# A hybrid state-space and attention layer: the u, gate and key products laid by hand as one stream of matmuls between the entry, the tables, the scan and the state outputs

## The chip, the cores and the metric

The kernel runs on one core of a Trainium2 chip. Five engines work side by side: TensorE (PE, matrix products), VectorE (DVE), ScalarE (ACT), GpSimd (POOL) and SyncE (SP, which here only starts DMA transfers). Each takes its own instructions in order, and semaphores hold an instruction back until what it needs is there. The metric is the device time of one execution in microseconds (us).

## The reference, cut to what matters

Two sequences of 512 tokens with 1024 features pass through one encoder layer. A state-space branch and a windowed attention branch are merged by two gates, and a squared-ReLU MLP follows.

```python
h = rms_norm(x, ln1)
q, k, v, u, g_att, g_ssm = split(h @ w_in)          # 1024, 256, 256, 1024, 1024, 1024 columns
k = rms_norm(k, k_gain)
# state-space branch: 64 groups of 16 channels, 64 states, two directions
a = exp(lam * dt);  bb = (a - 1) / lam * b           # complex
h_state[l] = a * h_state[l-1] + bb @ u[l]            # forward, and backward for the other direction
y = Re(c @ h_state), both directions, + d_skip * u
y_ssm = gelu(y) * sigmoid(gelu(y) @ w_glu + b_glu)
mixed = sigmoid(g_att) * y_att + sigmoid(g_ssm) * y_ssm
x = x + mixed @ w_out
out = x + square(relu(rms_norm(x, ln2) @ w_up)) @ w_down
```

## The kernel before, in words

Each fp32 operand of a large product is split into a high part and a rest (names ending in `_hi`, `_lo`, or `hT_0`, `hT_1`), and three products take the place of one. In what follows a "product" is one such matmul of 128x128 weights with 512 columns. A column of 128 output features costs 48 of them (8 slices of the inner dimension, three products each, two sequences). There are 24 columns: eight for u, eight for each gate. The keys take 192 matmuls with 256 columns.

**Entry.** For each of eight blocks of 128 rows: load, square and sum, normalise on DVE (`xn`, L152), turn with eight transposes (L157), split into `hT` (ACT L160, DVE L161). Among these stand some fifty small DVE operations that work out the powers of `a` (`exp_exact`, then `pr`, `pi`); ACT spreads these into `er`, `ei`, `br_p`, `bi_p`.

**Tables.** The 64 groups are done in eight blocks of eight groups (`tables(c)`), each block in two halves q of four groups. For each half DVE makes six operations for `bpre` (three each for real and imaginary part, L385 to L387) and six for `ctab` (L393 to L395). `ctab` goes to DRAM (L396). PE then has three pieces of work for each half: eight lag products of `lbt` with `ctab` (L404, each recorded as two matmuls, 48 output rows), whose results ACT copies to `ks` (L408); eight transposes of `bpre` (L417), copied to `bm` (L419); and eight state inputs `bm` with `u_sb` (L424, also recorded as two each), copied into `h` (L429, L430). `u_sb` (L412) is read back from `u_scr`, to which SP writes a finished u column in eight DMAs (L343). At the end of a block three DMAs store `ks` to `lag_scr` (L435 to L437). SP carries all these transfers in one queue, and the weight loads `c_raw` (L138) of the columns with them. The tile scheduler sets the order on every engine; a u column is emitted two blocks ahead of its tables.

**Scan.** 62 steps of four DVE operations on 128x256 (L533 to L536), each step needing the one before. PE meanwhile runs the gate columns that have no other place.

**State outputs.** 32 steps: copies of `h` into `st`, six logical matmuls (L561, L564), Gelu. From here the order on PE is written by hand: a generator (`gate_stream`, then `key_stream`) hands out products, 12 units after each step, a unit being half a product or one key matmul. What is left of the keys after the last step runs alone. The norm of each key tile follows on ACT, DVE, POOL and DVE (L518 to L524).

**Attention and the rest.** `kn` is read from the `keys` tiles in two DMAs (L806); the v weights `w_in` come in four DMAs (L797), and the query weights in others. The first matmuls of the attention stage stand at L646 and L664.

Of the kernel before, what the change touches and what calls it, by code (L numbers as in the profile page):

```python
# [12 lines left out]
F32 = mybir.dt.float32  # L13
# [50 lines left out]
def hybrid_layer(ctx, tc, x, rel, onehot, ln1, w_qkv, w_ug, q_gain, k_gain, sink, lam_re, lam_im, log_dt,  # L64
                 b_re, b_im, c_re, c_im, d_skip, w_glu, b_glu, w_out, ln2, w_up, w_down, out):
# [42 lines left out]
    bglu_sb = const.tile([P, KT], F32, name="bglu_sb")  # L108
    S.dma_start(bglu_sb, b_glu)
    gain_q = const.tile([P, 1], F32, name="gain_q")  # L110
    gain_k = const.tile([P, 1], F32, name="gain_k")
    S.dma_start(gain_q, q_gain)
    S.dma_start(gain_k, k_gain)
    V.tensor_scalar_mul(gain_q, gain_q, HD ** -0.5)
    nsink = const.tile([P, N_HEADS], F32, name="nsink")
    S.dma_start(nsink, sink.to_broadcast([P, N_HEADS]))
    V.tensor_scalar_mul(nsink, nsink, -1.0)

    def load_block(src, pool):

        hi = pool.tile([P, KT, CB], F32R, tag="w_hi", name="w_hi")
        lo = pool.tile([P, KT, CB], F32R, tag="w_lo", name="w_lo")
        for i in range(4):
            sl = slice(i * 2, i * 2 + 2)
            raw = wpool.tile([P, 2, CB], F32, tag="w_raw", name="w_raw")
            SP.dma_start(raw, src[:, sl, :])
            S.copy(hi[:, sl, :], raw)
            V.tensor_sub(lo[:, sl, :], raw, hi[:, sl, :].bitcast(F32))
        return hi, lo
# [13 lines left out]
    def rows_to_T(xt, gain_bc, pool, dst_hi, dst_lo, col):  # L143
# [8 lines left out]
        V.scalar_tensor_tensor(xn, xt, rs, gain_bc, op0=ALU.mult, op1=ALU.mult)  # L152
        for kq in range(KT // 4):
            ps = tps()
            for i in range(4):
                kk = kq * 4 + i
                PE.transpose(ps[:, i * P:(i + 1) * P], xn[:, kk * P:(kk + 1) * P], ident)  # L157
            psv = ps.rearrange("p (k t) -> p k t", k=4)
            h = dst_hi[:, kq * 4:kq * 4 + 4, col:col + P]
            S.copy(h, psv)  # L160
            V.tensor_sub(dst_lo[:, kq * 4:kq * 4 + 4, col:col + P], psv, h.bitcast(F32))  # L161
# [15 lines left out]
    def proj_rows(ps, w, act, col):  # L177

        for k in range(KT):
            mm3(ps, [t[:, k, col:col + P] for t in act], [t[:, k, :] for t in w], k == 0, k == KT - 1)  # L180

    def gate_column(c, scr, base):

        w = load_column(w_ug[base + c], V.tensor_sub)
        sg = evp.tile([P, NTOK], F32, tag="ev", name="sg")
        for s in range(NSEQ):
            ps = proj_T(w, 0, hT[s])
            S.activation(sg[:, s * HALF:(s + 1) * HALF], ps, AF.Sigmoid)
        SP.dma_start(scr[c], sg)

    def load_qkv(src):

        halves = []
        for e in range(2):
            hi, lo = [cpool.tile([P, KT // 2, CB], F32R, tag=tag, name=name) for tag, name in (("c_hi", "w_hi"), ("c_lo", "w_lo"))]
            for i in range(2):
                sl = slice(i * 2, i * 2 + 2)
                raw = cpool.tile([P, 2, CB], F32, tag="c_raw", name="w_raw")
                SP.dma_start(raw, src[:, e * 4 + i * 2:e * 4 + i * 2 + 2, :])
                S.copy(hi[:, sl, :], raw)  # L200
                V.tensor_sub(lo[:, sl, :], raw, hi[:, sl, :].bitcast(F32))
            halves.append((hi, lo))
        return halves
# [20 lines left out]
    dd = cf.tile([48, GROUPS], F32, name="dd")  # L224
    lbt = cf.tile([P, 2, SB, 48], F32, name="lbt")
    with tc.tile_pool(name="xin", bufs=2, reuse_waits="tile") as xin, tc.tile_pool(name="ssmc", bufs=1) as sc:
# [3 lines left out]
        lr, li, ldt = c64("lr"), c64("li"), c64("ldt")  # L230
        ln1_bc = xin.tile([P, D], F32, name="ln1_bc", bufs=1)
        SP.dma_start(ln1_bc, ln1.to_broadcast([P, D]))
        for t in range(NT):
            xt = xin.tile([P, D], F32, tag="xt", name="xt", bufs=6)
            SP.dma_start(xt, x[t * P:(t + 1) * P, :])
            rows_to_T(xt, ln1_bc, xin, hT[t // 4][0], hT[t // 4][1], (t % 4) * P)
            if t == 0:
                S.dma_start(lr, lam_re)
                S.dma_start(li, lam_im)
                for d in range(2):  # L240
                    S.dma_start(ldt[d * 64:(d + 1) * 64, :], log_dt[d:d + 1, :].to_broadcast([64, GROUPS]))
                SP.dma_start(dd[32:48, :], d_skip)
        V.memset(lbt, 0.0)
# [71 lines left out]
        for src, e_t, b_t in ((pr, er, br_p), (pi, ei, bi_p)):  # L315
# [4 lines left out]
            S.copy(b_t[64:128, :, :], src[64:128, 0:8, :])  # L320

    with tc.tile_pool(name="hst", bufs=1) as hp:
# [10 lines left out]
        def u_column(c):  # L335

            w = load_column(w_ug[U_BLK + c], V.tensor_sub)
            up = evp.tile([P, T, NSEQ, NCHUNK], F32, tag="ev", name="up")
            for s in range(NSEQ):
                ps = proj_T(w, 0, hT[s])  # L340
                S.copy(up[:, :, s, :], ps.rearrange("p (k t) -> p t k", t=T))
            for t in range(T):
                SP.dma_start(u_scr[t, :, c * 8:(c + 1) * 8].rearrange("c g k -> g c k"),  # L343
                             up[:, t].rearrange("p s k -> p (s k)"))

        with tc.tile_pool(name="ssmt", bufs=2) as sp:
            def tables(c):
# [3 lines left out]
                bx = sp.tile([P, 3, SB, CH], F32, tag="bx", name="bx")  # L351
                cx = sp.tile([P, 3, SB, CH], F32, tag="cx", name="cx")
                SP.dma_start(bx[:, 1], b_re[:, gs, :])
                SP.dma_start(bx[:, 2], b_im[:, gs, :])
                SP.dma_start(cx[:, 0], c_re[:, gs, :])
                SP.dma_start(cx[:, 1], c_im[:, gs, :])
                bb = sp.tile([P, 3, SB, CH], F32, tag="bb", name="bb", bufs=1)
                tw = sp.tile([P, 2, SB, CH], F32, tag="tb", name="tw", bufs=1)
                V.tensor_scalar_mul(bx[:, 0], bx[:, 2], -1.0)
                V.tensor_mul(tw, bx[:, 0:2], fi[:, None, gs, None].to_broadcast([P, 2, SB, CH]))  # L360
                V.tensor_mul(bb[:, 1:3], bx[:, 1:3], fr[:, None, gs, None].to_broadcast([P, 2, SB, CH]))
                V.tensor_add(bb[:, 1:3], bb[:, 1:3], tw)
                V.tensor_scalar_mul(bb[:, 0], bb[:, 2], -1.0)
                V.tensor_scalar_mul(cx[:, 1], cx[:, 1], -1.0)
                V.tensor_scalar_mul(cx[:, 2], cx[:, 0], -1.0)
                S.copy(lbt[0:64, :, :, 0:16], bb[0:64, 1:3])
                S.copy(lbt[64:128, :, :, 16:32], bb[64:128, 1:3])
                S.copy(lbt[:, :, :, 32:48], bb[:, 1:3])
                ks = sp.tile([48, SB, 9, CH], F32, tag="ks", name="ks", bufs=1)
                for q in range(SB // SG):  # L370
# [10 lines left out]

                    bpre = sp.tile([P, 2, SG, T, CH], F32, tag="bpre", name="bpre", bufs=1)
                    for ri in range(2):
                        tb = sp.tile([P, SG, 9, CH], F32, tag="tb", name="tb", bufs=1)
                        V.tensor_mul(bpre[:, ri], bc_pow(br_p, T), bc_ch(bb[:, 1 + ri], T))  # L385
                        V.tensor_mul(tb[:, :, 0:T, :], bc_pow(bi_p, T), bc_ch(bb[:, ri], T))
                        V.tensor_add(bpre[:, ri], bpre[:, ri], tb[:, :, 0:T, :])  # L387


                    ctab = sp.tile([P, SG, 2, 9, CH], F32, tag="ctab", name="ctab")  # L390
                    for ri in range(2):
                        tb = sp.tile([P, SG, 9, CH], F32, tag="tb", name="tb", bufs=1)
                        V.tensor_mul(ctab[:, :, ri], bc_pow(er, 9), bc_ch(cx[:, ri], 9))  # L393
                        V.tensor_mul(tb, bc_pow(ei, 9), bc_ch(cx[:, 1 + ri], 9))
                        V.tensor_add(ctab[:, :, ri], ctab[:, :, ri], tb)  # L395
# [4 lines left out]
                    for gp in range(SG // SH):  # L400
                        ps = sps()
                        for g in range(SH):
                            for ri in range(2):
                                PE.matmul(ps[0:48, g * 144:(g + 1) * 144], lbt[:, ri, q * SG + gp * SH + g, :],  # L404
# [36 lines left out]
            for c in range(KT):  # L441
                tables(c)
                if c + 2 < KT:
                    u_column(c + 2)
# [894 lines left out]
```

## Time and profile before

| what | us |
|---|---|
| median of three runs | 1583.43 (1581.27 to 1584.83) |
| the profiled execution | 1583.63 |
| its span in the profile | 1581.9 |
| PE busy in the span | 1499.1 |
| DVE busy | 1128.8 |
| ACT busy | 773.4 |

The span runs from the first to the last instruction, and 1.7 us of the profiled execution lie outside it. Busy time of PE counts an instruction until a modelled end, and consecutive matmuls overlap, so the number of matmuls times the distance between their starts is a better measure of PE's work than the busy sum. The stages by their first and last instructions: entry up to about 40 us, tables 60 to 231, scan 231 to 349, state outputs 349 to 449, the rest of the keys to 457.6. Between 40 and 60 us PE runs the first two u columns.

### The profile page before, as it was taken

To read this page: it belongs to the slowest core of one execution; us is meant where nothing else is said; L and a number is where in the kernel's file an instruction comes from. 1 tells how busy PE (TensorE), PEld (TensorE's weight loads), DVE (VectorE), ACT (ScalarE), POOL (GpSimd) and SP (SyncE) were. 2 spreads that over 40 slices of the span, in tenths; PEclk is the share of its full clock that TensorE was granted. 3 is DMA by queue.
4 is the path that set the end of the run, shared out by engine and by line. 5 is a ranking of instruction groups with operands and counts; after the bars stand their busy time and mean duration, and the time that the engine had idled before them with its cause. 6 is when DMAs were issued, how large, how long until landed. Compare 5 with 4: busy or idle time off the path is not lost.

```text
span 1581.9 us, 21603 instructions
## 1 busy us (share of the span) xinstructions
PE 1499.1 (95%) x7818; PEld 1261.1 (80%) x7818; DVE 1128.8 (71%) x2014; ACT 773.4 (49%) x1365; POOL 168.2 (11%) x294
## 2 busy tenths in 40 slices
PE   4999999999999999998699989999999899999999
PEld 3778878888999988986477777888888778888787
DVE  7899968994544978887866548777777478665553
ACT  5677662224434878787333325455544344433332
POOL 2000002002231233332320000000000000000000
PEclk9999999999999999999799998999999999999999
DMA  4444438626960412214754214444444594445332
GB/s 159 131 140 147 142 125 261 225 100 218 315 195 8 120 60 81 89 55 134 245 160 154 100 73 160 146 146 154 147 155 151 196 363 152 148 157 174 120 120 67
DMA packets 109558, 237.04 MB, mean 150 GB/s; under 512 B 15067, under 2 KB 37723, under 8 KB 109452
## 3 DMA queue, kind: packets, MB, share of 16 engines
q1 hardware_dynamic: 78988, 157.91, 31.2%
q0 software_dynamic: 11008, 39.89, 7.7%
q10 hardware_dynamic: 19456, 37.87, 6.5%
q8 instruction: 62, 1.02, 0.3%
q14 instruction: 44, 0.36, 0.1%
HBM read 165.34 MB, written 81.82 MB: 156 GB/s over the span
## 4 chain that ended last, share of the span: by engine, by line
PE 40%; issue 6%; DMA 2%; DVE 2%; POOL 2%; ACT 1%; POOLq 0%; ACTq 0%; SPq 0%; DVEq 0%
PE bank L166 13%; PE bank L167 13%; PE bank L165 13%; POOL mx L989 1%; PE acc L167 1%; PE acc L166 1%; PE acc L165 1%; DMA w_raw<-in_w_out_dram 0%; DMA k<-in_w_down_dram 0%; DMA fac<-rs_scr 0%; DMA mx<-ga_scr 0%; DVE rn_xn L1068 0%; ACT rn_xn L1064 0%; DMA mx<-mix_scr 0%; DMA mx<-gs_scr 0%
## 5 line engine op out<-in xcount | busy, mean ns | idle before, releaser
L165 PE MATMUL bank<-b_hi,a_hi 128*128 128x512 f32 x448 | 173.8, 391 | 7.3 <-ACT b_hi L1215 7.3
L166 PE MATMUL bank<-b_lo,a_hi 128*128 128x512 f32 x448 | 175.2, 391 | 2.1 <-DVE b_lo L1216 2.0
L167 PE MATMUL bank<-b_hi,a_lo 128*128 128x512 f32 x448 | 174.8, 390 | 0.0
L165 PE MATMUL bank<-act,act 128*128 128x512 f32 x376 | 147.1, 391 | 2.3 <-ACT act L1113 2.3
L1215 ACT CAST a_hi<-d_a 128x1024 fp32r<-128x1024 f32 x56 | 59.0, 1054 | 182.4 <-PE bank L166 175.3
L167 PE MATMUL bank<-act,act 128*128 128x512 f32 x376 | 146.8, 391 | 0.0
L166 PE MATMUL bank<-act,act 128*128 128x512 f32 x376 | 146.8, 390 | 0.0
L1216 DVE TENSOR_TENSOR a_lo<-d_a,a_hi 128x1024 fp32r<-128x1024 f32 x56 | 68.5, 1224 | 106.1 <-ACT a_hi L1215 106.1
L166 PE MATMUL acc<-hT,c_hi 128*128 128x512 f32 x336 | 133.7, 398 | 0.0
L165 PE MATMUL acc<-hT,c_hi 128*128 128x512 f32 x336 | 133.6, 398 | 0.0
L167 PE MATMUL acc<-hT,c_lo 128*128 128x512 f32 x336 | 132.4, 394 | 0.0
L664 PE MATMUL acc<-w_hi,hT 128*128 128x256 f32 x512 | 116.7, 296 | 0.0
L165 PEld LDWEIGHTS bank<-b_hi,a_hi 128*128 128x128 f32 x448 | 84.4, 189 | 25.2 <-ACT b_hi L1215 7.7
L166 PEld LDWEIGHTS bank<-b_lo,a_hi 128*128 128x128 f32 x448 | 84.4, 188 | 21.1 <-DVE b_lo L1216 3.6
L167 PEld LDWEIGHTS bank<-b_hi,a_lo 128*128 128x128 f32 x448 | 84.4, 188 | 17.5
L664 PEld LDWEIGHTS acc<-w_hi,hT 128*128 128x128 f32 x512 | 87.5, 190 | 3.8
L139 ACT CAST c_hi<-c_raw 128x512 fp32r<-128x512 f32 x64 | 39.4, 619 | 94.5 <-DMA c_raw<-in_w_ug_dram 39.8
L165 PEld LDWEIGHTS bank<-act,act 128*128 128x128 f32 x376 | 71.0, 189 | 17.3 <-ACT act L1113 2.7
L166 PEld LDWEIGHTS bank<-act,act 128*128 128x128 f32 x376 | 71.0, 189 | 14.8
L167 PEld LDWEIGHTS bank<-act,act 128*128 128x128 f32 x376 | 70.9, 189 | 15.0
L727 ACT ACTIVATE p<-p,nmx 128x257 f32<-128x257 f32 (+1 forms) x128 | 72.3, 565 | 15.4 <-DVE nmx L721 14.3
L1134 ACT ACTIVATE a<-a 128x512 f32<-128x512 f32 x64 | 40.5, 632 | 73.7 <-DVE a L1128 42.9
(309 smaller groups left out, 3771.7 us busy)
## 6 DMA issues: line engine op xcount, KB each, us to landing
d_a<-a_scr SPq DMA_DIRECT2D x56, 512.0 KB
u_raw<-in_w_up_dram SPq DMA_DIRECT2D x32, 512.0 KB
a_scr<-t ACTq DMA_DIRECT2D x64, 256.0 KB
k<-in_w_down_dram SPq DMA_DIRECT2D x32, 512.0 KB
c_raw<-in_w_ug_dram SPq DMA_DIRECT2D x48, 256.0 KB
a_scr<-a ACTq DMA_DIRECT2D x48, 256.0 KB
ct_scr<-ctab SPq DMA_DIRECT2D x16, 576.0 KB
ctab_in<-ct_scr POOLq DMA_DIRECT2D x16, 576.0 KB, 6.7
```

What stands on the lines that cost most here:

```text
L139: S.copy(hi[:, sl, :], raw)
L165: PE.matmul(ps, a[0], b[0], start=first, stop=False)
L166: PE.matmul(ps, a[0], b[1], start=False, stop=False)
L167: PE.matmul(ps, a[1], b[0], start=False, stop=last)
L664: PE.matmul(self.ps, hT[sq][act][:, k, col:col + P], w[:, k % 4, :], start=i == 0, stop=i == 3 * KT - 1)
L727: S.activation(p, p, AF.Exp, bias=self.nmx[:, h:h + 1], scale=-1.0, accum_out=self.sums[:, h, self.qb:self.qb + 1])
L989: GP.dma_start(t_, scr[m, :, s * HALF:(s + 1) * HALF])
L1134: S.activation(c, c, AF.Relu)
L1215: S.copy(hi, src)
L1216: V.tensor_sub(lo, src, hi.bitcast(F32))
```

## The change

The parameters arrive packed: `lam` (three rows of values) and `vec` (bias, gains, sink, skip) in one DMA each on ACT's queue, in place of eight or nine small ones. The skip values are placed on the host's side of the call as rows of the input array.

All 24 columns and the keys become one generator, `fillers`, and PE's order is by hand from the entry on. `pull(units)` takes so many units from it: 8 ahead of each half of the transposes of row blocks 4 to 7, 144 ahead of the tables, 52 in each half of a table block, 15 (eight products) in each scan step, then 32, and in the 32 state steps whatever is left, spread evenly.

In the tables DVE makes five operations for `bpre` and five for `ctab`, with sums and differences of the parts (`es`, `bs_p`, `bb[:, 2:4]`, `cw`) worked out once. The lag products write to output rows 0 to 63 and 64 to 127 in turn, into one PSUM bank, so that one copy of 128 partitions takes the place of two of 48. `lag_scr` is stored in twelve DMAs for each block instead of three. `u_sb` has one buffer instead of two. The line of relative biases moves into the scan. The number of gate columns whose sigmoid is applied on the spot stays 13.

```diff
-                    for gp in range(SG // SH):
-                        ps = sps()
-                        for g in range(SH):
-                            for ri in range(2):
-                                PE.matmul(ps[0:48, g * 144:(g + 1) * 144], lbt[:, ri, q * SG + gp * SH + g, :],
-                                          ctab[:, gp * SH + g, ri].rearrange("p n c -> p (n c)"),
-                                          start=ri == 0, stop=ri == 1)
-                        gk = q * SG + gp * SH
-                        S.copy(ks[:, gk:gk + SH].rearrange("p g n c -> p (g n c)"), ps[0:48, 0:SH * 144])
...
-                    u_sb = sp.tile([P, SI, NSEQ * NCHUNK], F32, tag="u_sb", name="u_sb")
+                    u_sb = sp.tile([P, SI, NSEQ * NCHUNK], F32, tag="u_sb", name="u_sb", bufs=1)
...
+                    pull(12)
+                    for gp, bm in enumerate(bms):
...
+                        pull(12 if gp == 0 else 16)
+                    ps = ps_o.tile([P, 512], F32, tag="po", name="lag")
+                    for g in range(SH):
+                        for ri in range(2):
+                            for e in range(2):
+                                gk = e * SH + g
+                                PE.matmul(ps[e * 64:(e + 1) * 64, g * 144:(g + 1) * 144], lbt[:, ri, q * SG + gk, :],
+                                          ctab[:, gk, ri].rearrange("p n c -> p (n c)"),
+                                          start=ri == 0, stop=ri == 1)
+                    S.copy(ks[:, q * SH:(q + 1) * SH].rearrange("p g n c -> p (g n c)"), ps[:, 0:SH * 144])
+                    pull(12)
...
-                SP.dma_start(lag_scr[:, gs, 8:15, :], ks[0:16, :, 0:7, :])
-                SP.dma_start(lag_scr[:, gs, 0:7, :], ks[16:32, :, 1:8, :])
-                SP.dma_start(lag_scr[:, gs, 7, :], ks[32:48, :, 8, :])
+                for e in range(2):
+                    kv = ks[e * 64:(e + 1) * 64].rearrange("p (q g) n c -> p q g n c", g=SH)
+                    for q in range(SB // SG):
+                        SP.dma_start(lv[e, :, q, :, 8:15, :], kv[0:16, q, :, 0:7, :])
+                        SP.dma_start(lv[e, :, q, :, 0:7, :], kv[16:32, q, :, 1:8, :])
+                        SP.dma_start(lv[e, :, q, :, 7, :], kv[32:48, q, :, 8, :])
-            u_column(0)
-            u_column(1)
+            pull(144)
             for c in range(KT):
                 tables(c)
...
                 V.tensor_add(h[:, i + 1], t1, t2)
+                pull(15)
...
-                room = 12
-                while room > 0:
-                    cost = next(stream, None)
...
+                pull(-(-phase["units"] // (GROUPS // SH - q)))
```

On SP, at the first table block, before: the u column 0 is stored, and the reads of `u_sb` for the first halves stand ahead of the store of u column 1.

```order
L343 DMA u_scr<-up 8x16x128 x8
L138 DMA c_raw<-in_w_ug_dram 128x512
L412 DMA u_sb<-u_scr 128x512 x2
L343 DMA u_scr<-up 8x16x128 x8
L396 DMA ct_scr<-ctab 128x1152
L412 DMA u_sb<-u_scr 128x512
```

The same place on SP now:

```order
L233 DMA u_scr<-up 8x16x128 x8
L119 DMA c_raw<-in_w_ug_dram 128x512
L233 DMA u_scr<-up 8x16x128 x8
L119 DMA c_raw<-in_w_ug_dram 128x512
L466 DMA ct_scr<-ctab 128x1152
L471 DMA u_sb<-u_scr 128x512
```

The first `u_sb` has moved behind the eight stores of column 1, a weight load and the store of the first `ctab`.

On SP, where the third table block (c = 2) begins, now: the twelve rows of the block before it, of which eight wait for its second half, stand ahead of this block's first `u_sb`. Before, the three rows stood in such a place too, with a second buffer to read into.

```order
L514 DMA lag_scr<-ks 16x2x112
L516 DMA lag_scr<-ks 16x2x16
L515 DMA lag_scr<-ks 16x2x112
L516 DMA lag_scr<-ks 16x2x16 x2
L514 DMA lag_scr<-ks 16x2x112
L515 DMA lag_scr<-ks 16x2x112
L516 DMA lag_scr<-ks 16x2x16
L466 DMA ct_scr<-ctab 128x1152
L471 DMA u_sb<-u_scr 128x512
```

The fourth block (c = 3) has the same arrangement; in the others `u_sb` stands ahead of them.

On SP, at the end of the keys, before, and then now:

```order
L806 DMA kn<-keys 128x1024
L797 DMA w_in<-in_w_qkv_dram 128x1024 x4
L806 DMA kn<-keys 128x1024
L631 DMA bias<-line_scr 128x384 x4
```

```order
L639 DMA w_raw<-in_w_qkv_dram 128x512 x2
L824 DMA kn<-keys 128x1024 x2
L815 DMA w_in<-in_w_qkv_dram 128x1024 x4
L649 DMA bias<-line_scr 128x384 x4
```

Both reads of `kn`, the second of which needs the last key tile, stand ahead of the four `w_in` loads now.

On PE, one half of a table block now (L478 are the transposes, L487 the state inputs, L500 the lag products, L212 the products of the columns; before, these three stood where the scheduler put them, in runs between products):

```order
L478 MATMUL tps<-ident,bpre 128x128 x8
L212 MATMUL acc<-hT_1_103,c_hi 128x512
L212 MATMUL acc<-hT_0_102,c_lo 128x512
L212 MATMUL acc<-hT_0_102,c_hi 128x512
L212 MATMUL acc<-hT_1_103,c_hi 128x512
L212 MATMUL acc<-hT_0_102,c_lo 128x512
L212 MATMUL acc<-hT_0_102,c_hi 128x512
L487 MATMUL sps<-u_sb,bm 128x128 x4
```

Six products follow these four state inputs, then the other four, eight products, the eight lag products and six products.

More of the change, by code (lines that the diff above doesn't have):

```diff
@@ L107, in hybrid_layer @@
     V.memset(neg_half, -0.5)
[L108 to L129, printed above, removed]
+    vec = const.tile([P, 58], F32, name="vec")
+    bglu_sb, gain_q, gain_k, nsink = [vec[:, a:b] for a, b in ((0, 8), (8, 9), (9, 10), (10, 26))]
+    dd = vec[:, 26:58].rearrange("p (x g) -> p x g", g=2)
     def load_column(src, sub):
@@ L152, in rows_to_T, with turn_rows @@
         V.scalar_tensor_tensor(xn, xt, rs, gain_bc, op0=ALU.mult, op1=ALU.mult)
[L153 to L161, printed above, removed]
+        return xn
+    def turn_rows(xn, kq, dst_hi, dst_lo, col):
+        ps = tps()
+        for i in range(4):
+            kk = kq * 4 + i
+            PE.transpose(ps[:, i * P:(i + 1) * P], xn[:, kk * P:(kk + 1) * P], ident)
+        psv = ps.rearrange("p (k t) -> p k t", k=4)
+        h = dst_hi[:, kq * 4:kq * 4 + 4, col:col + P]
+        S.copy(h, psv)
+        V.tensor_sub(dst_lo[:, kq * 4:kq * 4 + 4, col:col + P], psv, h.bitcast(F32))
     def mm3(ps, a, b, first, last):
@@ L175, in proj_T, with load_qkv_half @@
         return ps
[L177 to L203, printed above, removed]
+    def load_qkv_half(src, e):
+        hi, lo = [cpool.tile([P, KT // 2, CB], F32R, tag=tag, name=name) for tag, name in (("c_hi", "w_hi"), ("c_lo", "w_lo"))]
+        for i in range(2):
+            sl = slice(i * 2, i * 2 + 2)
+            raw = cpool.tile([P, 2, CB], F32, tag="c_raw", name="w_raw")
+            SP.dma_start(raw, src[:, e * 4 + i * 2:e * 4 + i * 2 + 2, :])
+            S.copy(hi[:, sl, :], raw)
+            V.tensor_sub(lo[:, sl, :], raw, hi[:, sl, :].bitcast(F32))
+        return hi, lo
     def slot(pool):
@@ new lines, in fillers, with pull @@
+    def fillers():
+        two = [column(i) for i in range(2)]
+        for parts, _ in two:
+            yield from parts[0]
+        for parts, store in two:
+            yield from parts[1]
+            store()
+            load_next()
+        for i in range(2, len(columns)):
+            parts, store = column(i)
+            for part in parts:
+                yield from part
+            store()
+            load_next()
+        yield from key_products()
+    filler = fillers()
+    def pull(units):
+        while units > 0:
+            cost = next(filler, None)
+            if cost is None:
+                return
+            units -= cost
+            phase["units"] -= cost
@@ L361, in tables @@
[L361 to L368, printed above, removed]
@@ L390, in tables @@
-                    ctab = sp.tile([P, SG, 2, 9, CH], F32, tag="ctab", name="ctab")
[L391 to L395, printed above, removed]
+                    tbb = tb[:, :, 0:T, :]
```

276 lines of the change are left out of this document (158 added, 118 removed).

## The prediction, on record before the changed kernel ran

> **What bounds the kernel now.** I read the page first, then the windows by stage, the groups of the tables stage, PE's waits there, and the timeline where stages meet.
>
> ```profile
> span 1581.9 us, 21603 instructions
> PE 1499.1 (95%) x7818; PEld 1261.1 (80%) x7818; DVE 1128.8 (71%) x2014; ACT 773.4 (49%) x1365; POOL 168.2 (11%) x294
> ```
>
> PE is the bound. The change can win only in the 83 us in which PE is idle, in the gaps that a busy share hides, or by making PE's work less. The windows give PE's busy time by stage and the clock granted to it:
>
> ```profile
> 0.00:20.00 20.00, 4.89 (x20) 3.71 (x20) 11.81 (x33) 10.39 (x19) 6.87 (x18) 1.00 0.80 273
> 20.00:40.00 20.00, 14.16 (x58) 11.33 (x57) 17.04 (x38) 11.28 (x20) 3.20 (x5) 0.83 0.16 46
> 60.00:231.00 171.00, 166.06 (x993) 135.16 (x994) 147.61 (x259) 123.24 (x181) 1.12 (x2) 1.00 0.47 147
> 231.00:349.00 118.00, 118.00 (x519) 96.78 (x518) 105.95 (x268) 23.32 (x42) 10.59 (x16) 1.00 0.57 193
> 349.00:458.00 109.00, 109.00 (x768) 101.40 (x767) 49.71 (x73) 42.52 (x78) 27.41 (x41) 1.00 0.71 242
> ```
>
> The columns are length, then busy time and instructions of PE, PEld, DVE, ACT and POOL, then clock, DMA share and GB/s. Scan and state outputs have no idle PE to win. The first 40 us have 21 us of it, the tables stage 4.9. How far matmuls stand apart tells the rest:
>
> ```profile
> 39.04 0.63 PE L167 MATMUL acc<-hT,c_lo 128*128 128x512 f32 x1
> 39.47 0.45 PE L165 MATMUL acc<-hT,c_hi 128*128 128x512 f32 x1
> ...
> 126.21 0.39 PE L165 MATMUL acc<-hT,c_hi 128*128 128x512 f32 x1
> ...
> 128.03 0.39 PE L167 MATMUL acc<-hT,c_lo 128*128 128x512 f32 x1
> 128.34 2.16 PE L404 MATMUL sps<-ctab,lbt 128*48 128x144 f32 x16
> 130.44 1.09 PE L417 MATMUL tps<-ident,bpre 128*128 128x128 f32 x8
> 131.29 0.48 PE L165 MATMUL acc<-hT,c_hi 128*128 128x512 f32 x1
> 131.77 2.05 PE L424 MATMUL sps<-u_sb,bm 128*128 128x128 f32 x16
> 133.66 0.49 PE L417 MATMUL tps<-ident,bpre 128*128 128x128 f32 x3
> ```
>
> Products from 126.21 to 128.03 are eight steps, 0.227 us each (0.43 from 39.04 to 39.47, while the clock was low). Sixteen recorded lag matmuls take 2.10 (128.34 to 130.44), eight transposes 0.85, sixteen state inputs 1.89 with the change of shape behind them (131.77 to 133.66). A change of shape costs: 0.08 from product to lag (0.31 less 0.227), 0.25 from product to state input (0.48 less 0.227).
>
> ```profile
> L166 PE MATMUL acc<-hT,c_hi 128*128 128x512 f32 x118 | 47.9, 406 | 0.0
> L404 PE MATMUL sps<-ctab,lbt 128*48 128x144 f32 x256 | 37.1, 290 | 3.1 <-ACT h L430 2.0 <-DVE ctab L395 1.1
> L424 PE MATMUL sps<-u_sb,bm 128*128 128x128 f32 x256 | 33.3, 282 | 2.4 <-ACT bm L419 2.1 <-ACT ks L408 0.2
> L417 PE MATMUL tps<-ident,bpre 128*128 128x128 f32 x128 | 18.9, 276 | 0.0
> L395 DVE TENSOR_TENSOR ctab<-ctab,tb 128x576 f32<-128x576 f32 x31 | 23.5, 757 | 0.8
> L387 DVE TENSOR_TENSOR bpre<-bpre,tb 128x512 f32<-128x512 f32 x30 | 20.6, 687 | 0.3
> ```
>
> So the tables stage holds some 354 products (3 x 118) at 0.227, 80.4 us; 16 x 2.10 = 33.6 of lag; 16 x 1.77 = 28.4 of state inputs (1.89 less the 0.12 of the change); 16 x 0.85 = 13.6 of transposes. That is 156 us in 171: 15 are lost, about 5.5 in the waits that the rows name, the rest in changes of shape and behind the waits.
>
> **The change, part by part.**
>
> *Entry.* DVE works out its powers first and normalises after that; parameters come in two DMAs. The same 20.9 us of large operations remain on DVE (8 x 1.28 and 16 x 0.69, below), but it starts sooner.
>
> ```profile
> 9.31 0.20 DVE L249 TENSOR_SCALAR ex_r<-ldt 128x64 f32<-128x64 f32 x1 [0.94 <-DMA ldt<-in_log_dt_dram]
> 11.58 1.28 DVE L152 SCALAR_TENSOR_TENSOR rn_xn<-xt,rs,ln_bc 128x1024 f32<-128x1024 f32 x1
> L161 DVE TENSOR_TENSOR hT<-tps,hT 128x512 fp32r<-128x512 f32 x16 | 10.6, 685 | 1.0 <-ACT hT L160 1.0
> ```
>
> Some 36 small operations at about 0.24, 8.6 us, stand ahead of the first `xn`. If `lam` lands near 4.5, `xn` begins near 13 instead of 11.58; but nothing small interrupts it after. I put the end of entry and first columns 3 us ahead: -3.0 (bounds: -4.5; +2 if `lam` lands near 7).
>
> *Tables, waits and shapes.* DVE drops two of twelve operations in each half, 16 x (0.69 + 0.76) = 23 us. That is cover, no path: PE's half is now 26 products (5.9), 2.10, 1.77 and 0.85, 10.6 us, against 7.8 of DVE (147.6 / 16 = 9.2, less 1.45). The 15 us lost go: -15.2. The new order pays its own changes of shape: 32 from product to state input and back at 0.25 + 0.04, 16 from product to lag and back at 0.08 + 0.10, 16 from product to transposes and back at 0.08: +13.5 (6 if most state inputs come without the 0.25).
>
> *Paired lag products.* Two output halves of 64 alternate. If two run at once, 33.6 us become 16.8. No row of this profile has such a pair; L404 uses 48 columns one after another. Bounds: 0 and -16.8; I take -16.8, since nothing but the array is shared by the two halves and their weights, sums and rows are apart. The Trainium skill, TensorEngine Tiling (Array Packing), Key Properties, says that tiles run independently, and that changing the tiling mode drains the array. By the first the saving would be the whole; by the second each return to products costs, and the trace agrees, with 0.08 us going in.
>
> *The first `u_sb`.*
>
> ```profile
> 52.78 5.07 SPq L343 DMA_DIRECT2D u_scr<-up  x8
> 59.23 0.34 SPq L138 DMA_DIRECT2D c_raw<-in_w_ug_dram  x1
> 59.81 0.81 SPq L412 DMA_DIRECT2D u_sb<-u_scr  x2
> 60.67 4.90 SPq L343 DMA_DIRECT2D u_scr<-up  x8
> ...
> 63.91 1.16 PE L424 MATMUL sps<-u_sb,bm 128*128 128x128 f32 x8 [0.23 <-ACT ks L408]
> 56.12 0.59 ACT L341 COPY up<-acc 128x512 f32<-128x512 f32 x1
> ```
>
> Eight stores occupy SP's queue 4.9 us, and now two lots of eight stand ahead. ACT's copy of u column 0 stands behind the `a8` block, near 56 as here; stores to 61.7, weight load, stores to 67, two more issues, `u_sb` at 68, landing at 71 to 72 (4.1 us from 59.81 to the use at 63.91). PE needed it at 63.91; 3 us of entry ahead, it is there at 60.9. That is +11 (6 if the copy comes five us sooner), and no product may pass it. After so long a wait PE starts again at low clock: seven or eight products at 0.43 instead of 0.227, +1.7. The Trainium skill, TensorE: Matmul & The Clock Gate, gives some 3.4 us of idling for the fall to half clock; the row with 0.83 and the 0.43 agree.
>
> *`u_sb` of blocks 2 and 3.* One buffer: its read can start only when the state inputs of the half before are through; in these two blocks the eight `lag_scr` rows in front also wait for that half's lag products, the copy to `ks` and DVE's addition.
>
> ```profile
> 76.96 0.33 SPq L435 DMA_DIRECT2D lag_scr<-ks  x1
> 77.34 0.43 SPq L436 DMA_DIRECT2D lag_scr<-ks  x1
> 77.81 0.44 SPq L437 DMA_DIRECT2D lag_scr<-ks  x1
> 78.76 0.34 SPq L412 DMA_DIRECT2D u_sb<-u_scr  x1
> ```
>
> From the last state input: eight products and the lag 4, copy and addition about 1 by an estimate (two operations like the 0.69 and 0.25 of other rows, on smaller tiles), eight issues at 0.39 3.1, one more 0.4: issue at 8.4, landing 3.5 to 4 later. PE needs it after 14 products, lag, transposes and six products, at 7.5 to 8. So +4.3 each: +8.5 (0 to 11). The six other blocks read ahead of the stores and come in time.
>
> *Scan.*
>
> ```profile
> L533 DVE TENSOR_TENSOR t<-h,a8r 128x256 f32<-128x256 f32 x62 | 26.3, 424 | 6.6 <-DMA c_raw<-in_w_ug_dram 4.7
> ```
>
> DVE needs the whole 118 us again, with its `c_lo` between; PE now has 496 products (112.4), and eight, the lag and six ahead of them and 16 behind. They meet within 2 us: +1.5 (0 to 3).
>
> *State outputs.* Keys are spread to 13.5 units a step and the tail of lone key matmuls goes; PE was full before, so this is worth nothing, covered by the same copies.
>
> *Tail.*
>
> ```profile
> 447.08 2.89 SPq L797 DMA_DIRECT2D w_in<-in_w_qkv_dram  x4
> 461.18 0.50 SPq L806 DMA_DIRECT2D kn<-keys  x1
> ...
> 457.81 0.37 PE L664 MATMUL acc<-w_hi,hT 128*128 128x256 f32 x1
> 461.81 0.39 PE L664 MATMUL acc<-w_lo,hT 128*128 128x256 f32 x1 [1.29 <-DVE w_lo L800]
> ```
>
> Before, `w_in` was issued 10 us ahead of the keys' end. Now it stands behind the `kn` read of 461.18, 3.4 us behind the first attention matmul at 457.81; with 0.5 for that issue and 4.1 to land and be used, as for `u_sb`, plus a cast, that matmul comes some 9 us late. Of the time to 461.81 before, about 2 were lost as well: +7 (4 to 9).
>
> Sum, from the profiled execution's own 1583.6 (0.2 above the median): -3.0 - 15.2 + 13.5 - 16.8 + 11 + 1.7 + 8.5 + 1.5 + 7 = +8.2, so **1591.8**, call it 1592.
>
> **The rivals.**
>
> *The lag halves don't overlap.* For it: what the trace shows of L404 runs strictly one after another, real and imaginary part, 0.13 us each, and no pair is in it. Then +16.8: 1608.6. It decides by the length of eight lag products, 2.1 or 1.05.
>
> *The `u_sb` loads come in time* (the other side). If DVE's early chain lets the copies of u columns 0 and 1 come near 50 to 52, and SP empties its queue faster than the two 5-us rows say, then the first state input finds its data, and in blocks 2 and 3 likewise: -11 - 1.7 - 8.5 gives 1570.6. Before, the one `u_sb` cost no wait (0.23 for ACT at 63.91), which is for it; the two lots of stores are against it. The point is whether `u_sb` is issued by 57.
>
> *The entry gets slower.* The first `xn` waits for `lam` and for a Sin of ACT in the chain ahead of it. If it starts at 17, entry ends 4 late: 1592 + 7 = 1599.
>
> **How the numbers follow.** Chances: forecast 0.45, no overlap 0.2, loads in time 0.22, slow entry 0.13. The forecast alone moves by its bounds about 8 either way, 1584 to 1600. The range 1571 to 1609 leaves out half of the outer two cases, about 0.2. Within 0.2% means within 3.2 us, about what a measurement of this kernel can tell from no change. Faster comes from the loads in time (0.2) and the low end of the others (0.06): 0.26. Same takes the edge of these, 0.08. Slower 0.66.
>
> **What would show it.** In the profile after: first `xn` near 13; eight lag products in 1.05; at the first L487 a wait of about 11 on a DMA, and two of about 4 some 40 and 60 us later; no DVE waits of PE in the tables; the first `w_hi` matmul about 9 us after the last key. The forecast is wrong if the lag cadence stays, if the waits at L487 are missing, or if a wait stands where I have none, above all between scan and state outputs.

## The result, and the profile after

The changed kernel takes 1673.05 us (median of four runs, 1667.72 to 1675.67) against 1582.43 before. The ratio is 1.0566, with a 95% interval of 1.0537 to 1.0596: 90 us slower, where 8 were forecast and the range ended at 1609. The profiled execution's span is 1673.6.

The waits of PE in the profile after, up to the attention stage (engine, tile and line, what was waited for: total us, times, longest):

```profile
PE acc L212 <- ACT sg L227: 61.9, 1, 61.9
PE sps L487 <- DMA u_sb<-u_scr: 20.6, 4, 10.2
PE tps L561 <- DMA rel_sb<-in_rel_dram: 13.3, 1, 13.3
PE tps L141 <- DVE rn_xn L133: 13.0, 1, 13.0
PE acc L682 <- ACT w_hi L817: 5.7, 1, 5.7
...
PE tps L664 <- POOL kd L655: 3.1, 1, 3.1
```

The waits at L487 and, at the start of the attention stage, at L664 and L682 were in the forecast. The first row and the third were not: 75.2 us, and both lie in the scan. The windows of the profile after show the place (length, then busy time and instructions of PE, PEld, DVE, ACT, POOL, then clock, DMA share, GB/s):

```profile
55.00:243.00 188.00, 167.42 (x1059) 138.55 (x1058) 129.51 (x241) 118.81 (x169) 0.00 (x0) 0.95 0.45 141
243.00:262.00 19.00, 15.71 (x68) 12.31 (x66) 13.50 (x34) 3.85 (x7) 7.52 (x11) 1.00 0.78 237
262.00:349.00 87.00, 18.23 (x66) 13.03 (x66) 83.18 (x219) 0.00 (x0) 2.65 (x5) 0.60 0.18 67
349.00:537.00 188.00, 184.91 (x1078) 161.74 (x1079) 59.01 (x86) 58.70 (x105) 26.71 (x41) 0.98 0.54 184
```

From 262 to 349 us DVE runs the scan almost without a break (83.18 of 87 us) while ACT does nothing at all (x0) and PE works 18 of 87 us. Before, PE had no idle time in the scan. ACT's own timeline says what it waits for:

```profile
257.16 0.59 ACT L227 ACTIVATE sg<-acc 128x512 f32<-128x512 f32 x1
257.65 0.61 ACT L120 CAST c_hi<-c_raw 128x512 fp32r<-128x512 f32 x1
349.06 2.01 ACT L578 COPY st<-h 64x512 f32<-64x512 f32 x2 [90.80 <-issue]
350.98 0.57 ACT L562 COPY ohln<-tps 16x512 f32<-16x512 f32 x1
351.46 0.58 ACT L227 ACTIVATE sg<-acc 128x512 f32<-128x512 f32 x1
351.94 0.60 ACT L120 CAST c_hi<-c_raw 128x512 fp32r<-128x512 f32 x1
```

The two copies of `h` into `st` are the first work of the state outputs. They need the last step of the scan, which ends at 349.0, and they stand in ACT's queue ahead of everything ACT still has to do for the products of the scan. So nothing empties the accumulators of the columns and nothing casts the next weights; PE fills what it has and stops. The row says "issue" because the semaphore wait is not resolved to a releaser there. The scan's last row on DVE, 348.48 with 0.43, ends just ahead of the copies:

```profile
348.48 0.43 DVE L557 TENSOR_TENSOR h<-t,t 128x256 f32<-128x256 f32 x1
```

ACT's order shows the same, and could be read before any run (dots stand for rows left out):

```
L227 ACTIVATE sg<-acc 128x512
...
L578 COPY st<-h 64x512
L578 COPY st<-h 64x512
L562 COPY ohln<-tps 16x512
L227 ACTIVATE sg<-acc 128x512
```

In the kernel before, all but a few of the scan's casts and sigmoids stand ahead of those copies, and ACT idles only 9.24 us in front of them:

```profile
339.17 0.62 ACT L139 CAST c_hi<-c_raw 128x512 fp32r<-128x512 f32 x1 [0.23 <-DMA c_raw<-in_w_ug_dram]
349.03 2.12 ACT L554 COPY st<-h 64x512 f32<-64x512 f32 x2 [9.24 <-DVE h L536]
```

What now stands between them is `ohln`, the copy behind the matmul of the relative biases (L561), which the change put into PE's order at scan step 8. The same matmul ran during the scan before, too, and cost no wait there: its table was loaded ahead of the scan, and its copy stood among the scan's own work on ACT. Rows of the kernel before, from SP, PE and ACT:

```profile
227.69 0.33 SPq L454 DMA_DIRECT2D rel_sb<-in_rel_dram  x1
245.15 1.03 PE L458 MATMUL tps<-oh_sb,rel_sb 33*16 33x512 f32 x2
246.21 0.58 ACT L460 COPY ln_sb<-tps 16x512 f32<-16x512 f32 x1 [6.59 <-PE tps L458]
```

Now SP issues that load at 260.00, when PE already waits for it:

```profile
260.00 0.67 SPq L544 DMA_DIRECT2D rel_sb<-in_rel_dram  x1
```

The lag products in pairs, on PE's timeline after:

```profile
160.12 0.39 PE L212 MATMUL acc<-hT,c_lo 128*128 128x512 f32 x1
160.44 1.20 PE L500 MATMUL lag<-ctab,lbt 128*64 128x144 f32 x16
161.57 0.74 PE L212 MATMUL acc<-hT,c_hi 128*128 128x512 f32 x2
```

Sixteen recorded matmuls, which are eight lag products, take 1.13 us (160.44 to 161.57) instead of 2.10.

### The profile page after: what moved, and what is told of

The parts are those of the page before. It is cut to its first block, busy times and chain, and to the rows that moved or that the text cites. A ratio compares the mean times of both kernels' runs of the same rounds, so it can differ in the third digit from the quotient of the medians.

```text
span 1673.6 us, 21682 instructions
## 1 busy us (share of the span) xinstructions
PE 1498.0 (90%) x7818; PEld 1256.0 (75%) x7818; DVE 1111.7 (66%) x1989; ACT 767.7 (46%) x1349; POOL 169.4 (10%) x298
## 4 chain that ended last, share of the span: by engine, by line
PE 37%; issue 6%; DMA 2%; DVE 2%; POOL 2%; ACT 1%; POOLq 0%; ACTq 0%; SPq 0%; DVEq 0%
PE bank L150 12%; PE bank L151 12%; PE bank L149 12%; POOL mx L1007 1%; DMA w_raw<-in_w_out_dram 0%; DMA mx<-mix_scr 0%; DMA mx<-ga_scr 0%; DMA k<-in_w_down_dram 0%; DVE rn_xn L1087 0%; DMA fac<-rs_scr 0%; DMA mx<-gs_scr 0%; ACT rn_xn L1083 0%; PE acc L151 0%; POOL rs L1086 0%; PE acc L150 0%
## 5 line engine op out<-in xcount | busy, mean ns | idle before, releaser
L212 PE MATMUL acc<-hT,c_hi 128*128 128x512 f32 x768 | 257.0, 410 | 61.9 <-ACT sg L227 61.9
L212 PEld LDWEIGHTS acc<-hT,c_hi 128*128 128x128 f32 x768 | 146.0, 193 | 94.5 <-ACT sg L227 62.3
L212 PE MATMUL acc<-hT,c_lo 128*128 128x512 f32 x384 | 157.6, 411 | 0.0
L682 PE MATMUL acc<-w_hi,hT 128*128 128x256 f32 x512 | 119.5, 301 | 5.7 <-ACT w_hi L817 5.7
L121 DVE TENSOR_TENSOR c_lo<-c_raw,c_hi 128x512 fp32r<-128x512 f32 x64 | 43.5, 689 | 95.5 <-ACT c_hi L120 95.1
L682 PEld LDWEIGHTS acc<-w_hi,hT 128*128 128x128 f32 x512 | 89.6, 195 | 9.6 <-ACT w_hi L817 5.9
L212 PEld LDWEIGHTS acc<-hT,c_lo 128*128 128x128 f32 x384 | 74.4, 194 | 17.6 <-issue 2.7
```

Of the source, the lines that this page charges most:

```text
L212: PE.matmul(ps, w[wi][:, k, :], hT[s][hi][:, k, :], start=n == 0, stop=n == 3 * KT - 1)
L682: PE.matmul(self.ps, hT[sq][act][:, k, col:col + P], w[:, k % 4, :], start=i == 0, stop=i == 3 * KT - 1)
```

## The experiments

Every ratio below is to the kernel before in runs on the same chip. The experiments ran on several chips, on which the medians of the kernel before lie between 1584.0 and 1584.7, so times of different runs are compared as they stand. The expectations name the runs by the order in which they ran: first the line of biases behind the scan, second step 20, third the shifted weights, fourth the lag products not alternating, sixth POOL's queue, seventh the tail, tenth all together with the line in the entry. "Theory A" is the reading above: the place of the bias matmul in PE's order makes the place of the state copies in ACT's.

**The line of biases behind the scan.**

```diff
-                if i == 8:
-                    ps = tps()
-                    PE.matmul(ps[0:N_HEADS, :], rel_sb, oh_sb, start=True, stop=True)
...
             pull(32)
+            ps = tps()
+            PE.matmul(ps[0:N_HEADS, :], rel_sb, oh_sb, start=True, stop=True)
```

> The line of relative biases (its matmul, ACT's copy and the two DMAs) is moved from scan step 8 to behind the scan; nothing else changes. Theory A (two state copies of ACT stand ahead of the scan's own ACT work because that matmul stands in PE's order at step 8): ACT works through the scan, the waits of 61.9 and 13.3 us go, and the time is 1673 - 75 - 2 of low clock = 1596, between 1590 and 1602. Rival B (ACT is held by the two buffers of the gate columns or by their stores on SP): the 61.9 us stay and only the 13.3 us go, 1660. Rival C (the wait for the relative table is itself the loss and the rest follows from low clock): like B, 1655 to 1660.

1604.55 us, ratio 1.0125 (1.0109 to 1.0142). Both waits are gone, 68 us of the 90 with them, so the rivals at 1655 to 1660 fall. The result is 3 us above theory A's band. One wait that neither kernel had is longer than that, from PE's waits in this run:

```profile
PE sps L584 <- DMA toep<-toep_scr: 10.2, 1, 10.2
```

**The same matmul at step 20.**

```diff
-                if i == 8:
+                if i == 20:
```

> The same matmul at scan step 20 instead of 8. Theory A: the two state copies move with it, so PE can run twelve more steps of eight products (22 us) before it starves; the 13.3 us wait for the table is gone too, since PE gets there later than 272 us. 1673 - 22 - 13 = 1638, between 1632 and 1645, with a wait of about 50 us that ends when the scan ends. Rivals B and C: no dependence on the step beyond the 13.3 us, 1660 in both places.

1654.19 us (two runs), ratio 1.0441 (1.0419 to 1.0462). From PE's waits:

```profile
PE acc L212 <- ACT sg L227: 49.5, 1, 49.5
...
PE tps L561 <- DMA rel_sb<-in_rel_dram: 6.3, 1, 6.3
```

The wait follows the step, as theory A says and the rivals do not, and its length of about 50 us was forecast. The forecast of the time was 16 us too low, and the upper end of its band 9: the wait shrank by 12.4 rather than 22, and the wait for the table by 7 rather than 13.3. Together 19.4 us, where the medians differ by 18.9. The load of the table moved along with the matmul, from 260.00 to 283.21, which is why that wait did not go. And here the row of the copies does name the scan as what ACT waits for:

```profile
283.21 0.42 SPq L544 DMA_DIRECT2D rel_sb<-in_rel_dram  x1
351.55 2.01 ACT L578 COPY st<-h 64x512 f32<-64x512 f32 x2 [71.07 <-DVE h L557]
```

In both runs the matmul in the scan also waits for its late table. A matmul at step 8 with the table loaded early was not tried, so the place alone and the place with the late load are not told apart.

**The line of biases at the end of the entry.**

```diff
+            if t == 3:
+                SP.dma_start(rel_sb[0:N_BUCKETS, :], rel)
+                SP.dma_start(oh_sb, onehot)
+        ps = tps()
+        PE.matmul(ps[0:N_HEADS, :], rel_sb, oh_sb, start=True, stop=True)
```

> The changed kernel with the line of relative biases worked out at the end of the entry instead of scan step 8: its two loads, matmul, copy and two DMAs stand there. Theory A: ACT's state copies stand behind the scan's work again, so the waits of 61.9 and 13.3 us go; and since line_scr (4 MB) is no longer written while the state outputs read their toep tiles, the wait of 10.2 us that the first run has at the state outputs goes too: 1604.5 - 10 - 1 = 1593, between 1590 and 1597. Rival H (the toep wait belongs to the new order of the state outputs and not to line_scr): it stays, 1604.

1592.05 us, ratio 1.0057 (1.0036 to 1.0079), as theory A said. The wait at the toep tiles is gone as well, so that cost belonged to my first edit, most likely because it had put the 4 MB write of `line_scr` beside the loads of the state outputs. The scan's window is full on PE, and ACT works in it:

```profile
262.00:349.00 87.00, 87.00 (x373) 69.96 (x372) 82.56 (x212) 16.41 (x29) 2.67 (x5) 1.00 0.45 159
```

So the misplaced line is worth 81 us (1673.05 to 1592.05), and the rest of the change is 0.6% slower than before. This run moves the load and the matmul together.

**Lag products not alternating.**

```diff
-                    for g in range(SH):
-                        for ri in range(2):
-                            for e in range(2):
+                    for e in range(2):
+                        for g in range(SH):
+                            for ri in range(2):
```

> As the first, but the four lag products of output rows 0 to 63 come first and then the four of rows 64 to 127, the same eight instructions in another order. Theory F (the halves run two at a time because neighbours lie in different halves): eight take 2.0 us or a little more instead of 1.13, so 16 x 0.9 = 14 us more than the first run. Rival G (the width of 64 or the shared bank makes them fast): no difference.

1612.46 us, ratio 1.0186 (1.0160 to 1.0211), 7.9 us more than the first run. The order alone makes the difference, so neighbours in different halves do run together and rival G falls. The size was off: on the timeline of this run the sixteen take 1.67 us (171.96 to 173.63), not 2.0. Their single starts in the trace show why: at both ends of the sixteen they stand 0.12 us apart, as the lag matmuls of 48 rows did before the change, and only over the seven distances around the change of half 0.06 on average, as everywhere when they alternate. So the width of 64 gains nothing by itself.

```profile
171.96 1.74 PE L500 MATMUL lag<-ctab,lbt 128*64 128x144 f32 x16
173.63 0.51 PE L212 MATMUL acc<-hT,c_lo 128*128 128x512 f32 x1
```

**Where the column weights lie.** In the profile after, products stand 0.234 us apart in every stage of the columns, against 0.227 before. Three runs lengthen a tile of constants, which moves the weights, and whatever else lies behind that tile, in memory. The addresses in what follows are worked out from the sizes of the tiles; no trace shows them. First by 32 bytes, on the kernel with the line behind the scan:

```diff
-    vec = const.tile([P, 58], F32, name="vec")
+    vec = const.tile([P, 66], F32, name="vec")[:, 0:58]
```

> As the first, and the tile of packed parameters is 8 floats longer, so that all column weights lie 32 bytes further (their address modulo 64 becomes 32, as that of the activations, as before the change). Theory D (a product costs 0.2345 us after against 0.2267 before because of where its weights lie): the steps are 0.2267 again and the time falls by 1152 x 0.0078 = 9.0 us against the first run. Rival E (the new order, or something of the run, makes products slower): 0.2345 stays, the same time within 1 us.

1605.09 us (ratio 1.0128, 1.0107 to 1.0148), and 0.233 on the timeline instead of 0.2267: theory D as put falls. Then the kernel before, shifted by 32 bytes:

```diff
-    nsink = const.tile([P, N_HEADS], F32, name="nsink")
+    nsink = const.tile([P, N_HEADS + 8], F32, name="nsink")[:, 0:N_HEADS]
```

> The kernel before, with one constant tile 8 floats longer, so that its column weights lie at 0 instead of 32 modulo 64 bytes. Nothing else differs. Theory D (the place of the weights against that of the activations sets the time of a product): 0.2345 instead of 0.2267 for the 1152 products, and up to 9 us slower, 1592. Rival E: no change, 1583.

1585.45 us, ratio 1.0006 (0.9997 to 1.0016). The whole time does not show it, but three of its products take 0.70 us:

```profile
262.14 0.40 PE L167 MATMUL acc<-hT,c_lo 128*128 128x512 f32 x1
...
262.84 0.40 PE L167 MATMUL acc<-hT,c_lo 128*128 128x512 f32 x1
```

Its first attention matmul starts at 461.91, where the kernel before has 457.81 (459.23 in the repetition below); the rest of the program makes up for that, and where it does was not looked into.

To exclude a difference between executions, the kernel before once more:

> The kernel before, unchanged, to see whether the distance of two products is the same in every execution. If 0.2267 belongs to the kernel, it is 0.2267 in the scan again. If it differs from execution to execution (the run with shifted weights showed 0.2333 at an unchanged time), it is nearer 0.234, and profiled times of stages carry that uncertainty of up to 3% on PE.

Its products in the scan, on the timeline of this run:

```profile
262.18 0.39 PE L167 MATMUL acc<-hT,c_lo 128*128 128x512 f32 x1
...
262.86 0.39 PE L167 MATMUL acc<-hT,c_lo 128*128 128x512 f32 x1
```

Three take 0.68 us here, 0.2267 each, as in its first profile (1587.1 us, one run), so the distance belongs to the kernel and not to the execution. The modulus of 64 was wrong. What fits all runs so far is that 0.2267 goes with byte 224 modulo 256, where the activations lie too, and 0.2333 to 0.2344 with 0, 64 and 96. The test of that follows below.

**`u_sb` from POOL's queue.**

```diff
-                    SP.dma_start(u_sb, u_scr[:, :, g0:g0 + SI]...
+                    GP.dma_start(u_sb, u_scr[:, :, g0:g0 + SI]...
```

> On the third run's kernel (line of biases behind the scan, weights shifted): the reads of u_sb in the tables are issued from POOL's queue instead of SP's. If SP's queue makes the waits at the state inputs, the 10.2 us of the first block fall to 3 to 5 (u_sb is issued when the eight stores of column 0 are done, near 58 to 59, and lands near 62), and those of 6.8 and 3.4 us in later blocks go to 0 to 2: 12 to 17 us faster than the third run. If the single buffer or the stores themselves make them, they stay.

1581.93 us, ratio 0.9988 (0.9979 to 0.9998), 23 us faster than the kernel it is made on. PE's waits between 55 and 250 us, of that kernel and of this one:

```profile
PE sps L487 <- DMA u_sb<-u_scr: 20.8, 4, 10.2
```

```profile
PE sps L487 <- DMA u_sb<-u_scr: 5.0, 1, 5.0
```

The queue made the waits, with one buffer as before. The gain is 7 us above the 15.8 us of waits that went. The starts of the transposes give part of it: above the 10.02 us of an undisturbed half, the halves of the tables lost 26 us in that kernel and lose 7 here, 19 us less, so low clock behind the waits is worth some 3. The other 4 were not found.

**The tail.**

```diff
+        SP.dma_start(kn[:, 0:4], key_tiles[0])
         w_q = whole_block(w_qkv[Q_BLK], ap, "ya", 2)
...
+        SP.dma_start(kn[:, 4:8], key_tiles[1])
...
-                pull(-(-phase["units"] // (GROUPS // SH - q)))
+                pull(12)
```

> On the third run's kernel: the second read of the keys is issued behind the four loads of w_in, and the state steps take 12 units each as before the change, so that the rest of the keys runs alone behind the last state step. Theory: the loads are issued when the state outputs end and the rest of the keys covers their landing; the two waits of 3.1 and 5.7 us at the start of the attention stage and the low clock behind them go: 8 to 10 us faster than the third run. Rival: w_in comes no earlier, since it waits for memory that the state stage holds; less than 3 us.

1597.65 us, ratio 1.0084 (1.0069 to 1.0099), 7.4 us less than the kernel it is made on. The two edits were made together and their shares are not known. SP's timeline shows `w_in` ahead of the second `kn`:

```profile
464.39 3.35 SPq L814 DMA_DIRECT2D w_in<-in_w_qkv_dram  x4
473.62 0.50 SPq L826 DMA_DIRECT2D kn<-keys  x1
```

**Together.** The three edits together, with the line behind the scan, then with the line in the entry and without the 32 bytes:

> The edits of the third, sixth and seventh runs together. If each acts by itself, the differences add: about 1587 - 14 - 9 = 1564, clearly faster than the kernel before (1583). If DVE becomes the bound in the scan (118 us for its 62 steps and the weight splits before), PE waits there for some 5 us: 1569.

> The line of biases in the entry, u_sb read from POOL's queue, the second read of the keys behind w_in and 12 units for each state step. If theory A holds with the toep wait as line_scr's doing: 1578 - 10 = 1568. If the toep wait stays: 1578.

1578.21 us (ratio 0.9960, 0.9946 to 0.9975), and 1568.97 us (0.9903, 0.9887 to 0.9919). The first is 14 us above its forecast, whose starting point was wrong: it took 1587 for a kernel that had run in 1605.09, toep wait included. From there the measured differences, 23.2 and 7.4, give 1574.5, so the edits nearly add up. The second meets its own forecast.

**Weights at byte 224 modulo 256**, on the second of these:

```diff
-    vec = const.tile([P, 58], F32, name="vec")
+    vec_all = const.tile([P, 98], F32, name="vec")
+    vec, dmask = vec_all[:, 0:58], vec_all[:, 58:74]
...
-    dmask = cf.tile([P, CH], F32, name="dmask")
```

> The tenth run's kernel with the constants 40 floats longer, so that the column weights lie at byte 224 modulo 256 of a partition, where they lay before the change and where the activations lie; the kernel with 0.2267 (224) and those with 0.2333 to 0.2344 (0, 64 and 96 modulo 256) differ in this too. Theory D2 (the place modulo 256 sets the time of a product): 0.2267 in the scan, and 1569 less up to 1152 x 0.0070 = 8 us: 1561 to 1566. Rival E2 (it is the order of the instructions): 0.233 again, 1569.

1564.06 us, ratio 0.9882 (0.9863 to 0.9902). Products of the scan, three of them apart, in the run that it is made on and in this one:

```profile
263.13 0.40 PE L212 MATMUL acc<-hT,c_lo 128*128 128x512 f32 x1
...
263.83 0.40 PE L212 MATMUL acc<-hT,c_lo 128*128 128x512 f32 x1
```

```profile
262.54 0.39 PE L212 MATMUL acc<-hT,c_lo 128*128 128x512 f32 x1
...
263.22 0.39 PE L212 MATMUL acc<-hT,c_lo 128*128 128x512 f32 x1
```

0.70 against 0.68 us for three: the same order of instructions at both distances, so rival E2 falls. The time is 4.9 us lower, but the intervals of the two ratios overlap, so the gain in time is likely and not shown.

**And the line of biases in the middle of the entry**, its DMAs on SP:

```diff
-        GP.dma_start(line_scr, line_one[:, None, :]...
+                SP.dma_start(line_scr, line_one[:, None, :]...
```

> As the run beside it, with the line of biases worked out in the middle of the entry and its two DMAs on SP's queue. If line_scr (4 MB), written near 40 to 60 us, is why the first u_sb is waited for 9.1 us instead of 4.8, the wait returns to 5 or less: 4 us less than the run beside it. If SP's stores of u are late behind line_scr now, it is no better or worse.

1560.11 us, ratio 0.9846 (0.9834 to 0.9859): the fastest, 24 us below the kernel before. The intervals of this run and the one beside it do not overlap. The place of the line and the queue of its DMAs changed together, so which of them gained the 4 us is not told apart. PE's wait for the first `u_sb`, in the run beside it and here:

```profile
PE sps L499 <- DMA u_sb<-u_scr: 9.3, 1, 9.3
```

```profile
PE sps L500 <- DMA u_sb<-u_scr: 5.6, 1, 5.6
```

## Why the prediction was wrong, and where it was right

**The step that failed is the scan.** It compared PE's products with DVE's steps, put +1.5 on them, and gave the line of biases, which the change moves in the program, no term and no reason for leaving it out. ACT, which stands between the two, was left out: its order has the two state copies ahead of the scan's casts and sigmoids. The price of that was 75.2 us of waits, and 81 us of time by the kernel with the line in the entry. An in-order queue has no small instruction; what counts is what is queued behind it. That the copies move with the matmul is shown (steps 8 and 20, behind the scan, in the entry). Why the scheduler puts them there was not tried; the late table is a candidate, since in the kernel before the same matmul ran in the scan at 245.15 us, with its table there, and the copies stayed behind the scan's work.

**The sum without that step** was 1591.8, and the kernel without the misplaced line takes 1592.05. That agreement is partly luck, as the terms show:

- *Entry*, -3.0. `xn` begins at 11.69 instead of the 13 I gave, and the tables' first transposes start at 55.83, behind 104 products; before, 96 were done by 60. Some 6 us, twice the term.
- *Waits of the tables*, -15.2 (171 less 156 is 15.0). No wait for DVE or ACT is left among PE's waits there, so the 5.5 us that the rows of before name are gone. The larger part, the changes of shape and what followed the waits, was not measured by itself.
- *Changes of shape*, +13.5. Mis-sized: from product to state input next to nothing is lost now (0.24 us from the last product at 165.12 to the state inputs at 165.36), where the row of before that I took showed 0.25. An undisturbed half takes 10.06 us (193.26 to 203.32), and its parts without any change of shape are 26 x 0.234 + 1.13 + 1.77 + 0.85 = 9.83. That leaves 0.23 for each of sixteen halves, about +4.
- *Pairs*, -16.8: 16 x 0.97 = -15.5. Right, and the rival with the halves one after another falls.
- *First `u_sb`*, +11 and +1.7: a wait of 10.2, and 11.9 with the low clock behind it (55.83 to 77.78, less 10.06). Right.
- *Blocks 2 and 3*, +8.5: waits of 6.8 and 3.4, on the state inputs of these two blocks. The wait is right, and the rival that held the loads to be in time falls, but the size is too small: these two halves are 9.4 and 5.0 us longer than an undisturbed one, 14.4 together, since low clock follows these waits too, and the forecast had none there.
- *Tail*, +7: waits of 3.1 and 5.7 with low clock behind them. The first `w_hi` matmul starts 9.7 us behind the last key, where about 9 were forecast, and the run with both tail edits gained 7.4. Right.
- *Missing*: products 3% apart, 1152 x 0.007 = 8 us of PE's time, with no row of before to show it.

With these sizes, and -15.2 and +1.5 as they were forecast, the sum is about +10, where the kernel without the misplaced line is 0.57% or 9 us slower than before. The entry, the changes of shape, the two blocks and the missing distance were each off by 3 to 10 us, and they cancelled.

The rows of these points on the timeline of the profile after, first PE's, in order of time (start of the tables, the loads of blocks 0, 2 and 3, the change of shape, the starts of two halves), then DVE's first `xn`:

```profile
55.83 1.04 PE L478 MATMUL tps<-ident,bpre 128*128 128x128 f32 x8
...
68.43 2.05 PE L487 MATMUL sps<-u_sb,bm 128*128 128x128 f32 x8 [10.16 <-DMA u_sb<-u_scr]
...
117.68 0.55 PE L487 MATMUL sps<-u_sb,bm 128*128 128x128 f32 x1 [6.80 <-DMA u_sb<-u_scr]
...
143.79 2.05 PE L487 MATMUL sps<-u_sb,bm 128*128 128x128 f32 x8 [3.38 <-DMA u_sb<-u_scr]
...
165.12 0.40 PE L212 MATMUL acc<-hT,c_lo 128*128 128x512 f32 x1
165.36 1.05 PE L487 MATMUL sps<-u_sb,bm 128*128 128x128 f32 x8
...
193.26 1.04 PE L478 MATMUL tps<-ident,bpre 128*128 128x128 f32 x8
...
203.32 1.04 PE L478 MATMUL tps<-ident,bpre 128*128 128x128 f32 x8
```

```profile
11.69 2.48 DVE L133 SCALAR_TENSOR_TENSOR rn_xn<-xt,rs,ln_bc 128x1024 f32<-128x1024 f32 x2
```

The prediction's own test, "if a wait stands where I have none, above all between scan and state outputs", names the failure. The range did not hold it, since no case in it had a stage stopped by an engine that was not in the sum.

## What to carry to other kernels

When one engine's order is laid by hand and the others' are left to a scheduler, read the order of all of them at each border of stages, and ask of every instruction that waits for the end of a stage what is queued behind it. Keep a small side computation out of a stage whose engines are all in step, or have its inputs there ahead of the stage: here it belonged in the entry. A transfer on the path should not share a queue with two lots of eight stores: from another engine's queue, with the single buffer kept, 15.8 of 20.8 us of waits went. A second buffer was not tried.

## What the runs showed of the hardware that was not expected

A matmul of 128x128 weights with 512 columns follows the one before after 0.2267 us when, by the sizes of the tiles, the weights lie at byte 224 modulo 256 of a partition, with the activations at 224 as well (two layouts, three kernels), and after 0.2333 to 0.2344 us when the weights lie at 0, 64 or 96. Whether it is the place itself or its equality with that of the activations was not told apart. In the kernel before the slower distance made no difference to the time beyond 0.16% (the upper end of the interval).

Eight lag products of 64 output rows took 1.13 us when neighbours lay in different halves and 1.67 us when four of one half came ahead of four of the other; those of 48 rows before, all in the same half, took 2.10 us. The order of issue decides how much of the overlap is had.
